# A decoder layer's feed-forward half: the sums and spills of its seven-product down projection on ScalarE's DMA queue, and a deeper buffer for its weights

## The chip, the cores and the metric

One of the eight cores of a Trainium2 chip runs the kernel. The metric is the time of one execution on the device, in microseconds (us). A core has TensorE (PE, matmuls), VectorE (DVE), ScalarE (ACT), GpSimd (POOL) and SyncE (SP). Each engine takes its instructions in a written order and waits on semaphores; transfers (DMAs) are issued here by SyncE and ScalarE, each in its own order, and run on sixteen DMA engines that all queues share.

## The reference

One decoder layer over 512 positions of width 1024: a mixer (mLSTM heads beside a gated convolution), then a feed-forward net whose hidden width is 2816. What the change touches is the end of the second half, here without the norms and the conditioning:

```python
up = causal_dwconv(u @ ffn_up[l], ffn_conv_w[l], ffn_conv_b[l])   # (512, 2 * 2816), three taps
a, gt = jnp.split(up, 2, axis=-1)
f = (jax.nn.silu(gt) * a) @ ffn_down[l]                           # (512, 2816) @ (2816, 1024)
x = x + g2 * rms_norm(f, ffn_post_g[l])
```

## The kernel before

All matmuls keep float32's accuracy by splitting both operands: ScalarE copies a 128x512 piece to a rounded high part (`hi`, line 182), and GpSimd or DVE subtracts it to get the low part (`lo`, line 183). `mm3` (line 201) then makes three matmuls for one product. `w_load` (line 190) loads 1 MB of weights by SyncE into one of two `raws` buffers and splits it into four pairs from `wpool` (20 buffers, so ten pairs).

**Up projection.** The loop over `i` runs over 22 tiles of 128 hidden channels. A tile needs four quarters of weights (`wup_0`, `wup_512`, `wup_1024`, `wup_1536`), has 48 matmuls (8 blocks of the inner dimension, three matmuls each, for two halves: the value `fa` and the gate `fg`), and ends in two PSUM banks of the four called `mm`. `conv3` (lines 969 and 971) makes the three-tap convolution, one tap on ScalarE and two on DVE; ScalarE takes the Silu of the gate (line 1043), DVE the product. The first three tiles are made earlier, in a code of their own; the loop's matmuls begin with tile 3. `u2h` and `u2l`, the split input of all up tiles, fill the buffers `uh` and `ul`.

**Down projection by seven products.** The first 18 hidden tiles go through Strassen's scheme (in Winograd's form): instead of eight products of blocks it makes seven, from sums of the blocks. A pair of hidden tiles gives the left operands: `x_` (`fx`), `r_` (`fr`) and their sums on GpSimd, `y_` (`fy`) and `q_` (`fq`). `q_` and half of `r_` are stored to device memory (`spills34`, `spilla22`) and read back later. For the right operands nine pieces of `w_down` (a list `AT` says at which up tiles) are loaded as four blocks `b` (`weight_load`), summed on DVE, GpSimd, DVE, GpSimd (`weight_sums`), and stored in `spillt1` to `spillt4` (`weight_store`). After the up projection `product` runs seven times, as p1, p2, p6, p5, p7, p3, p4: three loads of three pieces each by SyncE, then for each piece a split and 2 x 3 matmuls. `keep` copies a bank to SBUF on ScalarE (`kp`, `ku`), `put` adds it to another bank on DVE, and `back` reloads and splits `q_` (`s34`) and `r_` (`a22`). The last four hidden tiles (`wd`) are multiplied plainly, token tile by token tile, followed by the norm and the output.

**What sets the order.** SyncE and TensorE run in the order in which the code is written. For ScalarE, DVE and GpSimd a scheduler sets the order when the program is built, from its own estimate of when each operand will be ready; on the chip that order is fixed. A manual dependency of the kind `NoSync` only forces one instruction behind another on the same engine. So in the loop SyncE's queue holds, in this order, a tile's weight load, then `weight_load`, `weight_store` and the spills of earlier tiles, and a store waits there for its sum.

Of the kernel before, what the change touches and what calls it, by code (L numbers as in the profile page):

```python
# [10 lines left out]
F32 = mybir.dt.float32  # L11
F32R = mybir.dt.float32r
BF16 = mybir.dt.bfloat16
AF = mybir.ActivationFunctionType
# [3 lines left out]
P = 128  # L18
D = 1024
T = 512  # L20
KT = D // P
# [33 lines left out]
def decoder_layer(ctx, tc, w_glu0, x, c, adaT, vecs, w_glu, w_qko, w_v0, w_v, w_out, w_up, w_down, out):  # L55
    nc = tc.nc
    V, S, G, PE = nc.vector, nc.scalar, nc.gpsimd, nc.tensor
# [4 lines left out]
    raws = ctx.enter_context(tc.tile_pool(name="raws", bufs=RAWS))  # L62
    upool = ctx.enter_context(tc.tile_pool(name="upool", bufs=1))
# [24 lines left out]
    def slot(name, dt=F32):  # L88
        return slots.tile([P, T], dt, tag="t", name=name)

    def mmbank(name):
        return psum.tile([P, T], F32, tag="mm", bufs=4, name=name)
# [93 lines left out]
    def w_load(view, name, pool=None, tag="w"):  # L186

        n = view.shape[1]
        r = raws.tile([P, 2048], F32, tag="raw", name=name)
        nc.sync.dma_start(r[:, :n], view)  # L190
        return [w_split(r[:, a : min(a + T, n)], f"{name}_{a}", pool, tag) for a in range(0, n, T)]
# [105 lines left out]
    def u_tiles(name):  # L297
        hi = upool.tile([P, KT, T], F32R, tag="uh", name=f"{name}h")
        lo = upool.tile([P, KT, T], F32R, tag="ul", name=f"{name}l")
        return hi, lo, [(hi[:, j, :], lo[:, j, :]) for j in range(KT)]  # L300

    _, _, u = u_tiles("u")
# [397 lines left out]
    for j in range(KT):  # L700
# [4 lines left out]
        for d in range(1, SIDE + 1):  # L705
            t = cvs.tile([P, T], F32, tag="cvs", name=f"cs{j}_{d}")
# [134 lines left out]
    HT = T // 2  # L841
# [5 lines left out]
    def chain_sums(tt):  # L847

        ps = banks[tt]
        sq_sum(ps, msq[:, 2 * tt + 1 : 2 * tt + 2], f"mixb{tt}")  # L850
        un = adas.tile([P, D], F32, tag="ada", name=f"un{tt}")
        uns[tt] = [un[:, :T], un[:, T:]]
        V.tensor_tensor(out=uns[tt][1], in0=ps, in1=g1r[1], op=ALU.mult)
        return token_factor(msq[:, 2 * tt : 2 * tt + 2], f"rm{tt}")

    def chain_x(tt, r):

        xsq = small.tile([P, 2], F32, tag="xsq", name=f"xsq{tt}")
        for hf, m in enumerate((mg[tt], uns[tt][1])):
            V.scalar_tensor_tensor(out=x1[tt][hf], in0=m, scalar=r, in1=x1[tt][hf], op0=ALU.mult, op1=ALU.add)  # L860
            sq_sum(x1[tt][hf], xsq[:, hf : hf + 1], f"x1_{tt}_{hf}")
        for hf, un in enumerate(uns[tt]):
            V.tensor_tensor(out=un, in0=x1[tt][hf], in1=gs2r[hf], op=ALU.mult)
        return token_factor(xsq, f"rf{tt}")
# [36 lines left out]
    NE = 3  # L901
# [16 lines left out]
    with in_order():  # L918
# [3 lines left out]
        r = chain_sums(0)  # L922
        up_split(1, raw1, slots, "t")
        r = chain_x(0, r)
# [3 lines left out]
        r = chain_sums(1)  # L928
        up_split(1, raw1, slots, "t")
        r = chain_x(1, r)  # L930
# [4 lines left out]
        r = chain_sums(2)  # L935
        turn_out(1)
        r = chain_x(2, r)
# [4 lines left out]
        r = chain_sums(3)  # L942
        up_split(2, raw2, wpool, "w")
        r = chain_x(3, r)
# [29 lines left out]
    JP = 9  # L974
    NP = 2 * JP
    GJ = 3
    AT = [NE + 7 * j // 4 for j in range(JP)]
    spill = {q: dram.tile([P, JP * T], F32, tag=f"spill{q}", name=f"spill{q}") for q in ("t1", "t2", "t3", "t4", "s34", "a22")}
    sums = {}

    def weight_load(j):
        sums[j] = [slot(f"b{j}_{q}") for q in range(4)]
        for q, t in enumerate(sums[j]):
            nc.sync.dma_start(t, w_down[j][:, q * T : (q + 1) * T])

    def weight_sums(j):

        b11, b12, b21, b22 = sums[j]
        V.tensor_tensor(out=b11, in0=b12, in1=b11, op=ALU.subtract)  # L989
        G.tensor_tensor(out=b12, in0=b22, in1=b12, op=ALU.subtract)  # L990
        V.tensor_tensor(out=b22, in0=b22, in1=b11, op=ALU.subtract)
        G.tensor_tensor(out=b21, in0=b21, in1=b22, op=ALU.subtract)

    def weight_store(j):
        for q, t in zip(("t1", "t3", "t4", "t2"), sums.pop(j)):
            nc.sync.dma_start(spill[q][:, j * T : (j + 1) * T], t)

    f = {}
    af, asum, rest = [], [], []

    def split_f(src, name, wide):
        if wide:
# [8 lines left out]
    for i in range(NF):  # L1011
        if i < NE:
            pa, pg = early[i]
        else:
            pieces = w_load(w_up[i], f"wup{i}")
            if i in AT:
                weight_load(AT.index(i))
            if i - 2 in AT:
                weight_store(AT.index(i - 2))
            if i % 2 == 0 and 4 <= i < 4 + NP:  # L1020
                j = (i - 4) // 2
                x_, r_, q_ = rest[j]
                nc.sync.dma_start(spill["s34"][:, j * T : (j + 1) * T], q_)
                nc.sync.dma_start(spill["a22"][:, j * HT : (j + 1) * HT], r_[:, HT:])
            if i in (4, 8, 12, 16):
                ada_block(38 + i // 2, last_lo[0])
                ada_block(39 + i // 2, last_lo[0])
            if i == 19:
                ada_done(40, 48)
                gain(3, 40, "ffn_post_g")  # L1030
                send_rows(3 * KT, KT)
                wide = adas.tile([P, D], F32, tag="ada", name="g2r")
                g2r = row(3, lambda n: [wide[:, :T], wide[:, T:]], "g2")
            both = []
            for half in range(2):
                ps = mmbank(f"up{i}_{half}")
                for k in range(KT):
                    mm3(halves(ps), blk(pieces, half * KT + k), (u2h[:, :, k, :], u2l[:, :, k, :]), k == 0, k == KT - 1)
                both.append(ps)
            pa, pg = both  # L1040
        a = conv3(pa, i, f"fa{i}")
        g = conv3(pg, NF + i, f"fg{i}")
        S.activation(g, g, AF.Silu)
        if i >= NP:
            V.tensor_tensor(out=a, in0=a, in1=g, op=ALU.mult)
            f[i] = split_f(a, f"f{i}", False)
        else:
            if i % 2 == 0:
                x_, r_ = slot(f"fx{i}"), slot(f"fr{i}")
            cs = slice(i % 2 * HT, (i % 2 + 1) * HT)  # L1050
            V.tensor_tensor(out=x_[:, cs], in0=a[:, :HT], in1=g[:, :HT], op=ALU.mult)
            V.tensor_tensor(out=r_[:, cs], in0=a[:, HT:], in1=g[:, HT:], op=ALU.mult)  # L1052
            if i % 2:
                y_, q_ = slot(f"fy{i}"), slot(f"fq{i}")
                G.tensor_tensor(out=y_[:, :HT], in0=r_[:, :HT], in1=r_[:, HT:], op=ALU.add)  # L1055
                G.tensor_tensor(out=y_[:, HT:], in0=y_[:, :HT], in1=x_[:, :HT], op=ALU.subtract)
                G.tensor_tensor(out=q_[:, :HT], in0=x_[:, :HT], in1=r_[:, :HT], op=ALU.subtract)
                G.tensor_tensor(out=q_[:, HT:], in0=x_[:, HT:], in1=y_[:, HT:], op=ALU.subtract)
                af.append(split_f(x_, f"fx{i}", i == 1))
                asum.append(split_f(y_, f"fy{i}", i == 1))  # L1060
                rest.append((x_, r_, q_))
        if i in AT:
            weight_sums(AT.index(i))

    fsq = const.tile([P, 2 * NT], F32, name="fsq")
    banks = [[None, None] for _ in range(NT)]
    for tt, hf, make in [(2, 1, atbank), (3, 1, atbank), (0, 0, cvbank), (1, 0, cvbank), (0, 1, mmbank), (1, 1, mmbank), (2, 0, mmbank), (3, 0, mmbank)]:
        banks[tt][hf] = make(f"dn{tt}_{hf}")

    turn = [0]  # L1070

    def product(weights, left, th, hf, start, name):

        for a in range(0, JP, GJ):
            r = raws.tile([P, 2048], F32, tag="raw", name=f"{name}_{a}")
            view = weights(a)
            nc.sync.dma_start(r[:, : GJ * T].rearrange("p (j n) -> p j n", j=GJ), view)
            for n in range(GJ):
                j = a + n
                turn[0] += 1  # L1080
                w = w_split(r[:, n * T : (n + 1) * T], f"{name}_{j}", eng=V if turn[0] % 2 else G)
                hi, lo, off = left(j)
                for q in range(2):
                    ts = slice(off + q * P, off + (q + 1) * P)
                    mm3(banks[2 * th + q][hf], (hi[:, ts], lo[:, ts]), w, start and j == 0, j == JP - 1, True)
# [17 lines left out]

    def back(q, a, n, name):
        t = slot(f"{name}r")
        nc.sync.dma_start(t[:, :n], spill[q][:, a : a + n])
        hi, lo = slot(f"{name}h", F32R), slot(f"{name}l", F32R)
        S.activation(hi[:, :n], t[:, :n], AF.Copy)
        G.tensor_tensor(out=lo[:, :n], in0=t[:, :n], in1=hi[:, :n].bitcast(F32), op=ALU.subtract)
        return hi, lo  # L1110
# [7 lines left out]
    s34 = [back("s34", j * T, T, f"s34_{j}") for j in range(JP)]  # L1118
# [5 lines left out]
    a22 = [back("a22", a * HT, min(T, (JP - a) * HT), f"a22_{a}") for a in range(0, JP, 2)]  # L1124
# [9 lines left out]
    for tt in range(NT):  # L1134
# [12 lines left out]
        r = token_factor(fsq[:, 2 * tt : 2 * tt + 2], f"ro{tt}")  # L1147
# [70 lines left out]
```

## Time and profile before

| | |
|---|---|
| median of three runs | 861.71 us (861.38 to 867.46) |
| profiled execution | 867.5 us, of which the span is 865.8 us |
| mean granted clock of TensorE | 0.961 |
| busy: PE, DVE, ACT, POOL | 801.4, 526.7, 403.4, 499.4 us |
| DMA | 140.01 MB, mean 162 GB/s |
| SyncE's queue (q1) and ScalarE's (q10) | 116.26 and 23.08 MB |

In the rows of the profile a name such as `wup_0h<-wup` reads output <- input with buffer numbers left out, and `L182` is a line of the kernel. A row of the list of waits gives who waited, for whom, then us in total, how often, and the longest. A row of the timeline gives the start, the duration, the engine, the instruction, and in brackets the idle time before it and what ended it. A busy TensorE is not one at its peak, since its matmuls are pipelined; the distance between the starts of matmuls is what counts.

### The profile page before, as it was taken

How to read it: one execution, taken by the hardware profiler on the slowest of the kernel's cores; microseconds unless marked ns; L12 is line 12 of the kernel's file. 1: busy time of each engine (PE TensorE's matmuls, PEld its weight loads, DVE VectorE, ACT ScalarE, POOL GpSimd, SP SyncE). 2: the span in 40 equal slices, each digit the busy share in tenths (PEclk: the TensorE clock that was granted, in tenths of full speed). 3: DMA queues.
4: the chain of work that ended last, by engine and by line, in shares of the span. 5: the costliest groups of instructions: out<-in, count | busy, mean ns of one | idle time of the engine just before them, and what ended most of it. 6: DMA issues, size and time to landing. Idle time of an engine off the chain costs nothing.

```text
span 865.8 us, 10702 instructions
## 1 busy us (share of the span) xinstructions
PE 801.4 (93%) x3732; PEld 656.3 (76%) x3732; DVE 526.7 (61%) x824; ACT 403.4 (47%) x758; POOL 499.4 (58%) x414
## 2 busy tenths in 40 slices
PE   8999999999999999999999677797987899979996
PEld 5788887787888888888898565686766688858765
DVE  6679999999974345486877524535533335423334
ACT  6684466676645547423442233324233344544341
POOL 4799767786875325447131557357466482465661
PEclk9999999999999999999999788988989999998999
DMA  8953222121272315195367563345634353646444
GB/s 314 344 221 111 97 98 98 50 98 49 86 230 98 122 50 195 52 375 217 134 204 210 205 211 124 135 175 170 249 116 144 124 176 115 207 153 226 160 155 170
DMA packets 43897, 140.01 MB, mean 162 GB/s; under 512 B 4770, under 2 KB 6082, under 8 KB 37572
## 3 DMA queue, kind: packets, MB, share of 16 engines
q1 hardware_dynamic: 35748, 116.26, 38.4%
q10 hardware_dynamic: 8096, 23.08, 7.6%
q8 instruction: 29, 0.48, 0.2%
q14 instruction: 24, 0.20, 0.1%
HBM read 122.13 MB, written 17.19 MB: 161 GB/s over the span
## 4 chain that ended last, share of the span: by engine, by line
PE 65%; POOL 9%; issue 8%; DVE 8%; DMA 6%; ACT 4%; POOLq 0%; DVEq 0%; ACTq 0%; SPq 0%
PE up L201 18%; PE qko L201 12%; PE dn L201 8%; PE glu L201 6%; PE mixa L201 5%; PE mixb L201 5%; DMA ada<-in_adaT 3%; PE v L201 3%; PE s L513 2%; DVE cv L715 2%; PE o L524 1%; PE glu L344 1%; POOL wup_0l L183 1%; DMA p<-spillt 1%; DVE junk L167 1%
## 5 line engine op out<-in xcount | busy, mean ns | idle before, releaser
L715 DVE SCALAR_TENSOR_TENSOR cv<-gt,cvw,cv 128x502 f32<-128x502 f32 (+24 forms) x200 | 134.4, 727 | 1.9 <-ACT cv L703 1.3
L201 PE MATMUL up<-u2h,wup_0h 128*128 128x512 f32 (+1 forms) x100 | 43.7, 437 | 29.1 <-ACT wup_0h L182 29.1
L201 PE MATMUL up<-u2h,wup_0l 128*128 128x512 f32 (+1 forms) x100 | 44.6, 446 | 10.7 <-POOL wup_0l L183 10.7
L201 PEld LDWEIGHTS up<-u2h,wup_0h 128*128 128x128 f32 x100 | 22.6, 226 | 35.9 <-ACT wup_0h L182 32.5
L711 POOL TENSOR_TENSOR cs<-cs,cs 128x510 f32<-128x510 f32 (+3 forms) x32 | 42.7, 1337 | 4.7 <-ACT cs L709 4.7
L201 PE MATMUL up<-u2l,wup_0h 128*128 128x512 f32 (+1 forms) x100 | 42.6, 426 | 0.2 <-DVE u2l L884 0.2
L183 POOL TENSOR_TENSOR wup_0l<-wup,wup_0h 128x512 fp32r<-128x512 f32 x20 | 27.8, 1389 | 19.5 <-ACT wup_0h L182 19.5
L1055 POOL TENSOR_TENSOR fy<-fr 128x256 f32<-128x256 f32 x9 | 8.8, 978 | 51.9 <-DVE fr L1052 51.9
L201 PE MATMUL up<-u2h,wup_512h 128*128 128x512 f32 (+1 forms) x100 | 38.0, 380 | 0.0
L201 PE MATMUL up<-u2l,wup_512h 128*128 128x512 f32 (+1 forms) x100 | 37.5, 375 | 0.0
L201 PEld LDWEIGHTS up<-u2h,wup_0l 128*128 128x128 f32 x100 | 22.8, 228 | 19.2 <-POOL wup_0l L183 15.2
L201 PE MATMUL up<-u2h,wup_512l 128*128 128x512 f32 (+1 forms) x100 | 37.2, 372 | 0.0
L167 DVE SCALAR_TENSOR_TENSOR junk<-ada,cb 128x1024 bf16<-128x1024 f32 x20 | 29.2, 1459 | 12.1 <-DMA ada<-in_adaT 12.0
L201 PE MATMUL up<-u2h,wup_1024h 128*128 128x512 f32 (+1 forms) x100 | 36.4, 364 | 0.0
L201 PE MATMUL up<-u2h,wup_1536h 128*128 128x512 f32 (+1 forms) x100 | 36.4, 364 | 0.0
L201 PE MATMUL up<-u2l,wup_1536h 128*128 128x512 f32 (+1 forms) x100 | 36.4, 364 | 0.0
L201 PE MATMUL up<-u2h,wup_1024l 128*128 128x512 f32 (+1 forms) x100 | 36.4, 364 | 0.0
L201 PE MATMUL up<-u2h,wup_1536l 128*128 128x512 f32 (+1 forms) x100 | 36.3, 363 | 0.0
L201 PE MATMUL up<-u2l,wup_1024h 128*128 128x512 f32 (+1 forms) x100 | 36.3, 363 | 0.0
L183 POOL TENSOR_TENSOR wqko_1024l<-wqko,wqko_1024h 128x512 fp32r<-128x512 f32 x12 | 15.6, 1298 | 25.1 <-PE v L201 15.1
L990 POOL TENSOR_TENSOR b<-b,b 128x512 f32<-128x512 f32 x9 | 11.5, 1282 | 29.1 <-DVE b L989 29.1
L709 ACT ACTIVATE cs<-gt,cvw 128x511 f32<-128x511 f32 (+4 forms) x40 | 27.1, 712 | 1.5 <-POOL cs L711 1.0
(1024 smaller groups left out, 2772.4 us busy)
## 6 DMA issues: line engine op xcount, KB each, us to landing
wup<-in_w_up SPq DMA_DIRECT2D x22, 1024.0 KB, 5.2
wqko<-in_w_qko SPq DMA_DIRECT2D x12, 1024.0 KB, 4.8
ada<-in_adaT ACTq DMA_DIRECT2D x20, 512.0 KB, 5.5
b<-in_w_down SPq DMA_DIRECT2D x36, 256.0 KB, 6.6
spillt<-b SPq DMA_DIRECT2D x36, 256.0 KB, 2.0
p<-spillt SPq DMA_DIRECT2D x12, 768.0 KB, 5.5
ada<-in_adaT SPq DMA_DIRECT2D x16, 512.0 KB, 6.6
wo<-in_w_out SPq DMA_DIRECT2D x8, 1024.0 KB, 10.3
```

What stands on the lines that cost most here:

```text
L167: t = V.scalar_tensor_tensor(out=junk, in0=r, scalar=1.0, in1=cb, op0=ALU.mult, op1=ALU.mult, accum_out=mod[:, i : i + 1])
L183: (eng or G).tensor_tensor(out=lo[:, :n], in0=src, in1=hi[:, :n].bitcast(F32), op=ALU.subtract)
L201: PE.matmul(ps, l, r, start=start and i == 0, stop=stop and i == 2, skip_group_check=again)
L344: PE.matmul(ps, blk(wk, i)[a], u[k][b], start=k == 0 and p == 0, stop=k == KT - 1 and p == 1)
L513: PE.matmul(sp[:, :n], ks[d][:, cc * P : (cc + 1) * P], qs[d][:, cc * P :], start=d == 0, stop=d == 1)
L524: PE.matmul(o[:, : DH + 2], E[h][cc][:, a : a + P], vs[h][cc], start=cc == 0, stop=cc == tt)
L709: S.activation(t[:, d:], cvx[j][:, : T - d], AF.Copy, scale=w(CK - 1 - d))
L711: G.tensor_tensor(out=side[:, d:], in0=side[:, d:], in1=t[:, d:], op=ALU.add)
L715: last_tap = V.scalar_tensor_tensor(out=cp[:, d:], in0=cvx[j][:, : T - d], scalar=w(CK - 1 - d), in1=cp[:, d:], op0=ALU.mult, op1=ALU.add)
L990: G.tensor_tensor(out=b12, in0=b22, in1=b12, op=ALU.subtract)
L1055: G.tensor_tensor(out=y_[:, :HT], in0=r_[:, :HT], in1=r_[:, HT:], op=ALU.add)
```

## The change

The loads, stores and spills that belong to the seven products move from SyncE's queue to ScalarE's, each written at the place where its data arises and not two or more tiles later. `weight_load` is forced behind the last tile's Silu on ScalarE (`anchor`). `AT` becomes three tiles of every four from 6 to 16. `back` reloads through ScalarE's queue as well. `product` takes its first two loads into `raws` and all later ones into a ring of four buffers cut from `uh` and `ul`, which are free when the last up matmul has read `u2h` and `u2l`. The arithmetic is the same.

```diff
-    AT = [NE + 7 * j // 4 for j in range(JP)]
+    AT = [6, 7, 8, 10, 11, 12, 14, 15, 16]
+    def behind(ins, anchor):
+        tc.add_manual_dep(ins.ins, anchor.ins.name, mybir.DependencyInfo(mybir.DependencyClass.NoSync, mybir.DependencyReason.DATA),
+                          reason="order on an engine")
...
     def weight_load(j):
...
-            nc.sync.dma_start(t, w_down[j][:, q * T : (q + 1) * T])
+            behind(nc.scalar.dma_start(t, w_down[j][:, q * T : (q + 1) * T]), anchor[0])
...
     def weight_store(j):
         for q, t in zip(("t1", "t3", "t4", "t2"), sums.pop(j)):
-            nc.sync.dma_start(spill[q][:, j * T : (j + 1) * T], t)
+            nc.scalar.dma_start(spill[q][:, j * T : (j + 1) * T], t)
...
             if i in AT:
                 weight_load(AT.index(i))
-            if i - 2 in AT:
-                weight_store(AT.index(i - 2))
-            if i % 2 == 0 and 4 <= i < 4 + NP:
-                j = (i - 4) // 2
-                x_, r_, q_ = rest[j]
-                nc.sync.dma_start(spill["s34"][:, j * T : (j + 1) * T], q_)
-                nc.sync.dma_start(spill["a22"][:, j * HT : (j + 1) * HT], r_[:, HT:])
...
-        S.activation(g, g, AF.Silu)
+        anchor[0] = S.activation(g, g, AF.Silu)
...
-                rest.append((x_, r_, q_))
+                j = i // 2
+                nc.scalar.dma_start(spill["s34"][:, j * T : (j + 1) * T], q_)
+                nc.scalar.dma_start(spill["a22"][:, j * HT : (j + 1) * HT], r_[:, HT:])
         if i in AT:
             weight_sums(AT.index(i))
+            weight_store(AT.index(i))
...
-    turn = [0]
+    turn, at = [0], [0]
+    ring = [upool.tile([P, KT, T], F32, tag=tag, name=f"ring{tag}").rearrange("p j t -> p (j t)") for tag in ("uh", "ul")]
+    rings = [z[:, a : a + 2048] for a in (0, 2048) for z in ring]
...
-            r = raws.tile([P, 2048], F32, tag="raw", name=f"{name}_{a}")
+            r = rings[at[0] % len(rings)] if at[0] > 1 else raws.tile([P, 2048], F32, tag="raw", name=f"{name}_{a}")
+            at[0] += 1
...
     def back(q, a, n, name):
         t = slot(f"{name}r")
-        nc.sync.dma_start(t[:, :n], spill[q][:, a : a + n])
+        nc.scalar.dma_start(t[:, :n], spill[q][:, a : a + n])
```

How the built order moves is seen at three places. First SyncE in the middle of the up projection, from tile 11's weight load (`wup11`) on. Before, with the loads and stores of the sums (`b`, `spillt`) between the weight loads:

```order
L190 DMA wup11_5379<-in_w_up 128x2048
L984 DMA b5_0_5397<-in_w_down 128x512
L984 DMA b5_1_5398<-in_w_down 128x512
L984 DMA b5_2_5399<-in_w_down 128x512
L984 DMA b5_3_5400<-in_w_down 128x512
L190 DMA wup12_5484<-in_w_up 128x2048
L996 DMA spillt1_4528<-b4_0_5298 128x512
L996 DMA spillt3_4530<-b4_1_5299 128x512
L996 DMA spillt4_4531<-b4_2_5300 128x512
L996 DMA spillt2_4529<-b4_3_5301 128x512
L1023 DMA spills34_4532<-fq9_5267 128x512
L1024 DMA spilla22_4533<-fr8_5180 128x256
```

and in the change, from the same load:

```order
L190 DMA wup11_5369<-in_w_up 128x2048
L190 DMA wup12_5480<-in_w_up 128x2048
L190 DMA wup13_5585<-in_w_up 128x2048
L190 DMA wup14_5680<-in_w_up 128x2048
L190 DMA wup15_5777<-in_w_up 128x2048
```

Weight loads of the up projection now follow each other with nothing between.

Second, ScalarE around the split of tile 11's weights. Before, where the splits of tiles 11 and 12 (`wup11`, `wup12`) stand behind the convolution and the Silu of tile 10's gate (`fg10c`):

```order
L969 ACTIVATE fa10c_5362<-up10_0_5312,vec_108 128x512
L1007 ACTIVATE fy9h_5276<-fy9_5266 128x512
L969 ACTIVATE fg10c_5366<-up10_1_5337,vec_108 128x512
L1043 ACTIVATE fg10c_5366<-fg10c_5366 128x512
L182 ACTIVATE wup11_0h_5381<-wup11_5379 128x512
L182 ACTIVATE wup11_512h_5385<-wup11_5379 128x512
L182 ACTIVATE wup11_1024h_5389<-wup11_5379 128x512
L182 ACTIVATE wup11_1536h_5393<-wup11_5379 128x512
L182 ACTIVATE wup12_0h_5486<-wup12_5484 128x512
L182 ACTIVATE wup12_512h_5490<-wup12_5484 128x512
```

and in the change, from the first split of tile 11 on, with the loads (`b2`) of the third piece of weight sums:

```order
L182 ACTIVATE wup11_0h_5371<-wup11_5369 128x512
L989 DMA b2_0_5090<-in_w_down 128x512
L989 DMA b2_1_5091<-in_w_down 128x512
L989 DMA b2_2_5092<-in_w_down 128x512
L1061 DMA spills34_4532<-fq7_5049 128x512
L989 DMA b2_3_5093<-in_w_down 128x512
L969 ACTIVATE fg8c_5160<-up8_1_5131,vec_108 128x512
L182 ACTIVATE wup11_512h_5375<-wup11_5369 128x512
L1001 DMA spillt1_4528<-b2_0_5090 128x512
L182 ACTIVATE wup11_1024h_5379<-wup11_5369 128x512
```

The first split of tile 11 now stands ahead of tile 8's gate convolution, and the load and store of the sums stand among the splits; the store `spillt1` waits for DVE's first sum.

Third, ScalarE between the third product (p6) and the fourth (p5). Before, the splits of p5 stand behind the copies `ku20` and `ku21`, which need p6's last matmul:

```order
L1096 ACTIVATE ku20_6729<-dn2_1_6427 128x512
L1096 ACTIVATE ku21_6730<-dn3_1_6428 128x512
L1108 ACTIVATE s34_6h_6771<-s34_6r_6769 128x512
L1108 ACTIVATE s34_7h_6777<-s34_7r_6775 128x512
L1108 ACTIVATE s34_8h_6783<-s34_8r_6781 128x512
L182 ACTIVATE p5_0h_6789<-p5_0_6787 128x512
L182 ACTIVATE p5_1h_6799<-p5_0_6787 128x512
L182 ACTIVATE p5_2h_6809<-p5_0_6787 128x512
```

and in the change, from p5's fifth piece to p7's first:

```order
L182 ACTIVATE p5_4h_6824<-ringuh_6435 128x512
L1111 DMA s34_4r_6752<-spills34_4532 128x512
L182 ACTIVATE p5_5h_6834<-ringuh_6435 128x512
L182 ACTIVATE p5_6h_6845<-ringul_6436 128x512
L1113 ACTIVATE s34_4h_6754<-s34_4r_6752 128x512
L182 ACTIVATE p5_7h_6855<-ringul_6436 128x512
L1111 DMA s34_5r_6758<-spills34_4532 128x512
L182 ACTIVATE p5_8h_6865<-ringul_6436 128x512
L1101 ACTIVATE ku20_6724<-dn2_1_6427 128x512
L182 ACTIVATE p7_0h_6880<-ringuh_6435 128x512
```

All of p5's splits now stand ahead of the copies, and the reloads of s34 and their splits are spread among them.

More of the change, by code (lines that the diff above doesn't have):

```diff
@@ L995, in weight_store @@
         for q, t in zip(("t1", "t3", "t4", "t2"), sums.pop(j)):
-            nc.sync.dma_start(spill[q][:, j * T : (j + 1) * T], t)
+            nc.scalar.dma_start(spill[q][:, j * T : (j + 1) * T], t)
     f = {}
-    af, asum, rest = [], [], []
+    af, asum = [], []
+    anchor = [None]
     def split_f(src, name, wide):
```

## The prediction

> **What bounds the kernel now.** I read the page first, for the engine that carries the chain, then the stages of the feed-forward half, then the waits of TensorE there, then one wait in order of time.
>
> ```profile
> span 865.8 us, 10702 instructions
> ...
> PE 65%; POOL 9%; issue 8%; DVE 8%; DMA 6%; ACT 4%; POOLq 0%; DVEq 0%; ACTq 0%; SPq 0%
> ```
>
> TensorE has most of the chain, but a third of it lies elsewhere. The next view gives the busy time by stage: first to last matmul of up tiles 3 to 21, the seven products, the first 9.9 us of the closing products, the rest, and last a stretch of two up tiles without a wait.
>
> ```profile
> 464.30:735.40 271.10, 231.28 (x915) 183.86 (x914) 120.91 (x168) 97.61 (x161) 152.06 (x130) 0.90 0.47 163
> 735.40:832.50 97.10, 88.88 (x380) 72.17 (x378) 37.05 (x38) 45.59 (x82) 57.45 (x42) 0.96 0.57 194
> 832.50:842.40 9.90, 7.74 (x26) 3.90 (x25) 1.57 (x3) 3.28 (x7) 9.26 (x8) 1.00 0.20 80
> 842.40:865.80 23.40, 16.48 (x73) 13.31 (x71) 11.32 (x19) 5.18 (x16) 2.19 (x4) 0.93 0.46 157
> 603.30:625.00 21.70, 21.70 (x98) 17.96 (x97) 11.68 (x16) 7.04 (x11) 12.14 (x12) 1.00 0.76 274
> ```
>
> The columns are the stretch, its length, the busy us (and instructions) of TensorE, its weight loads, DVE, ScalarE and GpSimd, then granted clock, DMA share and GB/s. No other engine is near full in the up stage, and the DMA engines are half idle (0.47). The last row shows that TensorE can run there without a gap at clock 1.00 while 274 GB/s move. So it is held by waits, and TensorE's own waits name them:
>
> ```profile
> PE up L201 <- ACT wup_0h L182: 29.1, 8, 4.2
> PE up L201 <- POOL wup_0l L183: 10.7, 8, 5.5
> PE dn L201 <- POOL p_0l L183: 5.5, 2, 3.9
> PE dn L201 <- ACT p_0h L182: 2.8, 1, 2.8
> ```
>
> Eight times an up tile's first quarter of weights isn't split when TensorE comes to it. Tile 11 stands for all eight (rows of SyncE, ScalarE, TensorE and GpSimd in order of time, with the page's landing time for such a load):
>
> ```profile
> wup<-in_w_up SPq DMA_DIRECT2D x22, 1024.0 KB, 5.2
> ...
> 566.51 0.33 SPq L190 DMA_DIRECT2D wup<-in_w_up  x1
> 587.17 0.78 ACT L969 ACTIVATE fg10c<-up,vec 128x512 f32<-128x512 f32 x1 [3.69 <-PE up L201]
> 589.61 0.63 ACT L1043 ACTIVATE fg10c<-fg10c 128x512 f32<-128x512 f32 x1 [1.66 <-DVE fg10c L971]
> 590.15 0.61 ACT L182 ACTIVATE wup_0h<-wup 128x512 fp32r<-128x512 f32 x1
> 586.75 0.39 PE L201 MATMUL up<-u2h,wup_1536l 128*128 128x512 f32 x1
> 590.81 0.80 PE L201 MATMUL up<-u2h,wup_0h 128*128 128x512 f32 x1 [3.68 <-ACT wup_0h L182]
> 592.93 0.80 PE L201 MATMUL up<-u2h,wup_0l 128*128 128x512 f32 x1 [0.90 <-POOL wup_0l L183]
> 604.97 0.39 PE L201 MATMUL up<-u2h,wup_0h 128*128 128x512 f32 x1
> 615.85 0.39 PE L201 MATMUL up<-u2h,wup_0h 128*128 128x512 f32 x1
> ```
>
> The load was issued at 566.51 and, at 5.2 us, had landed by 572. ScalarE split it at 590.15, 18 us later: in its written order the split stands behind tile 10's second convolution and its Silu, which end only after tile 10's matmuls. The wait is one of order, not of transfer. It costs more than its 3.68 us: tile 11 takes 604.97 - 590.81 = 14.16 us, and the next, without a wait, 615.85 - 604.97 = **10.88 us**.
>
> **The change, part by part.** *Up stage.* SyncE keeps only the weight loads of the up projection there; the 72 loads and stores of the sums and the 18 spills go to ScalarE's queue. With that the scheduler writes ScalarE's splits elsewhere: tile 11's first split now stands ahead of tile 8's second convolution, more than two tiles before TensorE needs it. All 19 tiles at 10.88 us are 206.7 us; the stage took 271.1. Gain if no wait is left: **64.4 us**, eight times 8.05 (39.8 / 8 = 5.0 waited, the rest lost at the lowered clock, 0.90 over the stage).
>
> What it adds to ScalarE is issuing. The nearest rows on its queue (min/median/max of an issue in ns), the landing times, and the other engines' shares in the sums:
>
> ```profile
> L960 ACTq DMA_DIRECT2D x1d<-x x8: 326/327/333, 413.2 to 436.8; - x8
> L826 ACTq DMA_DIRECT2D x<-in_x x8: 334/442/489, 368.4 to 376.7; - x8
> ...
> x<-in_x ACTq DMA_DIRECT2D x8, 256.0 KB, 6.1
> b<-in_w_down SPq DMA_DIRECT2D x36, 256.0 KB, 6.6
> spillt<-b SPq DMA_DIRECT2D x36, 256.0 KB, 2.0
> L183 POOL TENSOR_TENSOR wup_512l<-wup,wup_512h 128x512 fp32r<-128x512 f32 x18 | 24.3, 1352 | 0.0
> L989 DVE TENSOR_TENSOR b<-b,b x9: 682/686/1771, 479.0 to 677.2; 128x512 f32<-128x512 f32 x9
> L990 POOL TENSOR_TENSOR b<-b,b 128x512 f32<-128x512 f32 x9 | 11.5, 1282 | 29.1 <-DVE b L989 29.1
> L1055 POOL TENSOR_TENSOR fy<-fr 128x256 f32<-128x256 f32 x9 | 8.8, 978 | 51.9 <-DVE fr L1052 51.9
> ```
>
> Between 0.33 and 0.44 us an issue; I take 0.44, that of several in a row. A tile with sums then asks ScalarE for four splits at 0.6, two convolutions at 0.78, a Silu and a split of the product at 0.63, together 5.3 us, and nine issues, 4.0 us: 9.3 of 10.88 us. Nine of the tiles 6 to 17 have sums, three need only some 5.7. GpSimd has four splits at 1.35, half a pair's sums (four operations of at most 0.98 for two tiles, 2.0) and two weight sums at 1.28: 10.0 at most with sums, 7.4 without, 112 of 131 us over the twelve. Both fit, without much room.
>
> The new waits stand at ScalarE: a store waits for DVE's or GpSimd's sum, and the first sum for loads that ScalarE issued a few instructions before. Behind that store stand the next splits, the convolution and the Silu; DVE waits for the convolution (and holds its own next convolution behind the sum that waits for the load), TensorE for the split two tiles on. A load lands in 2.0 (the bound below, from the store row) to 6.6 us, with two to four instructions in between. That leaves 0 to 4 us of waiting a tile, and I take 2, nearer to 6.1 less some 4: 11.3 us a tile with sums. Over twelve tiles that is 9 x 0.4 late and 3 x 5 of slack, so no lasting delay. At 4 us it is 9 x 2.4 = 22 less 15, a lag of 7. Two leads cover a lag: ten quarters of split weights (wpool's 20 buffers, 27 us of matmuls), and the PSUM banks of two tiles, which leave a convolution a tile and a half, 16 us. I charge nothing; without the cover each late tile costs some 8 us as now.
>
> That the sums now start at tile 6 and not 3 leaves the first three tiles without them; the last store, about tile 18, is read by the third product, over four tiles later.
>
> Bandwidth: the stage's 163 GB/s over 271 us are 44 MB; in 207 us, 214 GB/s, below the 274 that ran beside matmuls at full rate.
>
> *Products.* The second part in order of time:
>
> ```profile
> 735.41 0.39 PE L201 MATMUL dn<-p_0h,fx 128*128 128x512 f32 x1
> 747.69 0.39 PE L201 MATMUL dn<-p_0h,fx 128*128 128x512 f32 x1
> 771.80 1.28 ACT L1096 ACTIVATE ku<-dn 128x512 f32<-128x512 f32 x2 [9.97 <-PE dn L201]
> 774.53 0.62 ACT L182 ACTIVATE p_0h<-p 128x512 fp32r<-128x512 f32 x1
> 779.58 0.79 PE L201 MATMUL dn<-p_0l,fy 128*128 128x512 f32 x1 [3.88 <-POOL p_0l L183]
> 807.93 0.50 PE L201 MATMUL dn<-p_0l,s_0h 128*128 128x512 f32 x1 [1.58 <-POOL p_0l L183]
> 832.48 0.39 PE L201 MATMUL dn<-wd_0h,f18h 128*128 128x512 f32 x1
> 842.39 0.39 PE L201 MATMUL dn<-wd_0h,f18h 128*128 128x512 f32 x1
> 847.84 0.39 PE L201 MATMUL dn<-wd_0h,f18h 128*128 128x512 f32 x1
> ```
>
> One product is 747.69 - 735.41 = 12.28 us (1.36 for each of nine pieces), seven are 86.0; they took 832.48 - 735.41 = 97.1. Lost: **11.1 us**, most of it where p5's splits stand behind the copies ku, which wait 9.97 us for the end of a product. In the new order all nine splits of p5 stand ahead of those copies, and four ring buffers besides two keep loads ahead. The ring is free only when the last up matmul ends, so the third load starts then; TensorE has six pieces in hand, 6 x 1.36 = 8.2 us, against some 4.4 to 6.6 for the landing and 1.9 for a split (0.62 on ScalarE, 1.28 on GpSimd). Covered; without the cover a short wait. The reloads of s34 and a22 make ScalarE wait at their splits, a few us each at most, while its splits may run ten pieces (13.6 us) ahead.
>
> *Closing products.* The first token tile took 842.39 - 832.48 = 9.91 us, the second 5.45: GpSimd was still splitting wd (busy 9.26 of 9.90 in the stage view). These loads now go to buffers that have been free since the first product, and their splits are paced by p4's matmuls. Gain: **4.5 us**. What is late next is nothing but TensorE; the tail after it stays.
>
> *Sum.* The profiled execution took 867.5 us, of which 1.7 lies around the span. 867.5 - 64.4 - 11.1 - 4.5 = 787.5. I add 1.6 for one short wait like that at 807.93: **789 us**. That execution is the slowest of the three shown; the median is 861.71, so 5.8 us of it may be no part of the kernel's usual time, and the result may as well be 783.
>
> **Rivals.** *ScalarE falls behind* (chance 0.15): loads on its queue land later than 6.6 us or GpSimd's sums hold the stores, the lead is used up by tile 12, and four of the later tiles wait. At 2.4 us of delay and 3.3 for the clock (14.16 less 10.88) each, 23 us: 811. For it: the 9.3 of 10.88 us. Against it: three tiles of slack.
>
> *Only the up stage gains* (0.10): the reloads' waits at ScalarE take the place of the copies' wait in the products: 787.5 + 11.1 + 1.6, 800.
>
> *No change* (0.03): both queues feed the same transfers, loads land no sooner, and the splits stay late: 862 to 867. Against it: the 18 us between landing and split. The Trainium skill, "DMA: Bandwidth & Descriptors", section "Issuing engines are not separate DMA queues", speaks for this rival: issuing from several engines saves only the sequencer's time. By that rule the sum would be near 0, since SyncE's issuing is on no path; the trace doesn't contradict it on bandwidth, but bandwidth isn't what TensorE waits for.
>
> *Slower* (0.04): each of the nine tiles with sums makes ScalarE wait out its own chain: load, four sums, store. With nothing between, that is 9.3 + 6.6 + 3.9 (two sums on DVE at 0.68 and two on GpSimd at 1.28) = 19.8 us a tile, 8.9 above 10.88, and 3.3 for the clock: nine times 12.2 is 110, and 787.5 + 110 = 897. It decides against the change from (80 - 9 x 3.3) / 9 = 5.6 us above 10.88, that is 16.5 us a tile.
>
> **How the numbers follow.** Forecast 0.68 (783 to 795), the rivals 0.15, 0.10, 0.03 and 0.04. The range goes from 779 (783 less the doubt of 4 in the terms) to 812, which takes in both smaller gains. Faster by over 1%, about what a measurement of this kernel can tell from no change: 0.68 + 0.15 + 0.10 = 0.93; within 1%: 0.03; slower: 0.04.
>
> **What would show it.** In the trace after, TensorE's waits for wup_0h and wup_0l should be gone or below 5 us in sum, up tiles 3 to 21 should last about 207 us at clock 1.00, the products 86 to 88, the first closing tile 5.5. ScalarE should wait for DVE and GpSimd at the stores, some 2 us a tile. Waits of TensorE from tile 12 on, growing, would mean the first rival; a wait at s34's or a22's split the second.

## The result

The changed kernel takes 790.64 us (median of four, 789.48 to 792.1), the kernel before 861.91 in the same session (861.38 to 867.46): a ratio of 0.916, 95% interval 0.912 to 0.920. The forecast was 789.

The page of the changed kernel, its span and its chain of work:

```profile
span 788.9 us, 10687 instructions
...
PEclk9999999999999999999999999999999999999999
...
PE 78%; DVE 9%; DMA 6%; ACT 3%; issue 2%; POOL 1%; ACTq 0%; DVEq 0%; SPq 0%; POOLq 0%
```

TensorE's share of the chain went from 65 to 78%, GpSimd's from 9 to 1, that of "issue" from 8 to 2, and the granted clock stays at nine tenths or more in every slice. The stages, with the columns that the prediction explains (up tiles 3 to 21, seven products, first closing token tile, rest):

```profile
464.42:674.16 209.74, 207.40 (x915) 171.15 (x914) 130.47 (x164) 93.02 (x152) 152.10 (x126) 1.00 0.61 203
674.16:760.07 85.91, 85.91 (x380) 70.95 (x378) 48.26 (x43) 50.04 (x91) 71.10 (x49) 1.00 0.72 247
760.07:765.51 5.44, 5.44 (x26) 4.50 (x24) 1.38 (x3) 0.00 (x0) 2.17 (x2) 1.00 0.00 0
765.51:788.90 23.39, 16.48 (x73) 13.33 (x71) 11.52 (x20) 5.51 (x16) 2.21 (x4) 0.92 0.46 157
```

Against 271.1, 97.1, 9.9 and 23.4 us in the profiled execution of the kernel before (its slowest, 867.46 us), the stages gain 61.4, 11.2, 4.5 and nothing. TensorE, 231.28 us busy in the up stage before, is now 207.40 for the same matmuls: the waits had cost time in the matmuls too, at a granted clock of 0.90. Its waits after 440 us are only two, of another kind than before:

```profile
PE up L201 <- DVE fa17c L971: 1.2, 1, 1.2
PE up L201 <- DVE fa15c L971: 1.2, 1, 1.2
```

Tile 11, the prediction's example, in order of time (ScalarE, then TensorE):

```profile
531.65 0.62 ACT L182 ACTIVATE wup_0h<-wup 128x512 fp32r<-128x512 f32 x1
534.53 0.78 ACT L969 ACTIVATE fg8c<-up,vec 128x512 f32<-128x512 f32 x1 [2.26 <-issue]
551.49 0.39 PE L201 MATMUL up<-u2h,wup_0h 128*128 128x512 f32 x1
```

Its first split stands ahead of tile 8's second convolution and is made 19.8 us before TensorE comes for it; before, it came 0.66 us ahead of a matmul that had waited 3.68 us.

### The profile page after: what moved, and what is told of

Read it like the earlier page. It is cut to its first block, busy times and chain, and to the rows that moved or that the text cites. A ratio compares the mean times of both kernels' runs of the same rounds, so it can differ in the third digit from the quotient of the medians.

```text
span 788.9 us, 10687 instructions
## 1 busy us (share of the span) xinstructions
PE 772.3 (98%) x3732; PEld 643.1 (82%) x3732; DVE 550.5 (70%) x824; ACT 403.6 (51%) x758; POOL 511.8 (65%) x414
## 4 chain that ended last, share of the span: by engine, by line
PE 78%; DVE 9%; DMA 6%; ACT 3%; issue 2%; POOL 1%; ACTq 0%; DVEq 0%; SPq 0%; POOLq 0%
PE up L201 26%; PE dn L201 13%; PE qko L201 10%; PE glu L201 7%; PE mixa L201 6%; PE mixb L201 5%; PE glu L344 4%; DVE cv L715 4%; PE v L201 3%; DMA b<-in_w_down 2%; PE s L513 2%; DMA ada<-in_adaT 1%; PE o L524 1%; DMA wqko<-in_w_qko 1%; DMA vec<-in_vecs 1%
## 5 line engine op out<-in xcount | busy, mean ns | idle before, releaser
L201 PE MATMUL up<-u2h,wup_0h 128*128 128x512 f32 (+1 forms) x100 | 36.6, 366 | 2.3 <-DVE fa17c L971 1.2
L201 PE MATMUL up<-u2l,wup_0h 128*128 128x512 f32 (+1 forms) x100 | 36.5, 365 | 0.2 <-DVE u2l L884 0.2
L167 DVE SCALAR_TENSOR_TENSOR junk<-ada,cb 128x1024 bf16<-128x1024 f32 x20 | 32.0, 1599 | 6.5 <-DMA ada<-in_adaT 6.3
L201 PE MATMUL up<-u2h,wup_0l 128*128 128x512 f32 (+1 forms) x100 | 36.4, 364 | 0.0
L201 PE MATMUL up<-u2h,wup_512h 128*128 128x512 f32 (+1 forms) x100 | 36.4, 364 | 0.0
L183 POOL TENSOR_TENSOR wup_0l<-wup,wup_0h 128x512 fp32r<-128x512 f32 x20 | 27.4, 1369 | 11.2 <-ACT wup_0h L182 11.2
L183 POOL TENSOR_TENSOR wup_1024l<-wup,wup_1024h 128x512 fp32r<-128x512 f32 x20 | 26.7, 1335 | 10.8 <-ACT wup_1024h L182 10.8
L183 POOL TENSOR_TENSOR wup_512l<-wup,wup_512h 128x512 fp32r<-128x512 f32 x20 | 27.4, 1369 | 8.0 <-ACT wup_512h L182 8.0
L182 ACT ACTIVATE wup_0h<-wup 128x512 fp32r<-128x512 f32 x22 | 13.8, 627 | 34.7 <-POOL b L995 11.0
L183 POOL TENSOR_TENSOR wup_1536l<-wup,wup_1536h 128x512 fp32r<-128x512 f32 x20 | 28.6, 1432 | 3.2 <-PE up L201 2.2
```

Source lines behind the costliest of these rows:

```text
L167: t = V.scalar_tensor_tensor(out=junk, in0=r, scalar=1.0, in1=cb, op0=ALU.mult, op1=ALU.mult, accum_out=mod[:, i : i + 1])
L182: S.activation(hi[:, :n], src, AF.Copy)
L183: (eng or G).tensor_tensor(out=lo[:, :n], in0=src, in1=hi[:, :n].bitcast(F32), op=ALU.subtract)
L201: PE.matmul(ps, l, r, start=start and i == 0, stop=stop and i == 2, skip_group_check=again)
```

## The experiments

### The up stage: the queues, or the order they bring about

The queues changed and with them ScalarE's written order. Two runs part the two; a third keeps only the loads on SyncE. The edits are shown in short, with `...` where code is left out. First, the new queues with the old order:

```diff
 pieces = w_load(w_up[i], f"wup{i}")        # wacts: the splits on ScalarE
...
+if i % 2 and i >= 5:
+    behind(wacts[0], anchor[0])
```

> The changed kernel with every transfer on the queue that the change gave it, but the first split of each odd up tile from 5 on pinned on ScalarE behind the Silu of the tile before, which makes ScalarE's written order that of the kernel before (two tiles' splits in a row, then two tiles' convolutions). Theory (order of the splits is the cause, the queues only bring it about): the waits for wup_0h are back, eight or nine of them at 7 to 8 us each, up tiles 3 to 21 take 262 to 275 us, products and closing stay at 86 and 5.4, total 843 to 858. Rival (the transfers run better from two queues, order matters little): up tiles 209 to 220 us, total 790 to 801.

Measured: 863.6 us, ratio to before 0.9996 (0.9976 to 1.0016). The time is that of the kernel before, some 6 us above the theory's 858. TensorE's waits, the stages (up, products, closing), and tile 11 again (ScalarE, DVE and TensorE in order of time):

```profile
PE up L203 <- ACT wup_0h L184: 39.4, 9, 5.6
PE up L203 <- POOL wup_0l L185: 12.0, 8, 2.8
```

```profile
464.59:747.21 282.62, 231.13 (x916) 182.69 (x914) 119.78 (x166) 95.17 (x153) 147.07 (x125) 0.89 0.44 150
747.21:833.11 85.90, 85.90 (x379) 70.95 (x378) 46.24 (x41) 50.44 (x90) 74.07 (x52) 1.00 0.71 247
833.11:838.55 5.44, 5.44 (x25) 4.50 (x24) 1.38 (x3) 0.00 (x0) 1.02 (x1) 1.00 0.00 0
```

```profile
578.63 0.78 ACT L971 ACTIVATE fg10c<-up,vec 128x512 f32<-128x512 f32 x1 [3.68 <-DMA b<-in_w_down]
579.65 0.69 DVE L996 TENSOR_TENSOR b<-b,b 128x512 f32<-128x512 f32 x1 [3.52 <-issue]
580.26 1.53 DVE L973 SCALAR_TENSOR_TENSOR fg10c<-up,vec,fg10c 128x511 f32<-128x511 f32 x2
581.88 0.63 ACT L1047 ACTIVATE fg10c<-fg10c 128x512 f32<-128x512 f32 x1 [2.47 <-DVE fg10c L973]
582.41 0.61 ACT L184 ACTIVATE wup_0h<-wup 128x512 fp32r<-128x512 f32 x1
583.08 0.79 PE L203 MATMUL up<-u2h,wup_0h 128*128 128x512 f32 x1 [4.49 <-ACT wup_0h L184]
```

The split stands behind the Silu again, and TensorE waits 4.49 us. The up stage takes 282.6 us, more than the 271.1 of before and than the theory's 262 to 275, and this takes back what products and closing keep of the change. The waits for wup_0h are 39.4 us against 29.1. There are nine and not eight, and the chain behind some of them is longer: at tile 10 DVE makes a sum of weights (0.69 us) ahead of the gate's two taps, the Silu waits 2.47 us for DVE and not 1.66, and TensorE's wait is longer by the same 0.81 us.

Then the other way round: the old queues, tiles of sums and buffers, with the splits early.

```diff
+for n in (i + 1, i + 2):                   # from tile 4 on
+    if n < NF and n not in ahead and i >= 4:
+        ahead[n] = w_load(w_up[n], f"wup{n}"); heads[n] = list(wacts)
...
 a = conv3(pa, i, f"fa{i}")
-g = conv3(pg, NF + i, f"fg{i}")
+g = conv3(pg, NF + i, f"fg{i}", heads[i + 2][0])   # pinned behind this split
```

> The kernel before with all its queues, its tiles of sums and its buffers, but the load and splits of an up tile written two tiles ahead, and the second convolution of each tile pinned on ScalarE behind the first split of the tile two later. Theory (order): the 18 us between landing and split go, up tiles 3 to 21 take 207 to 222 us, the products (97) and the closing stage (9.9) stay, total 798 to 815. Rival (SyncE's queue itself holds the loads back, since stores wait in it): the loads land late and ScalarE now waits for them ahead of its convolutions, up tiles 245 us or more, total 836 to 880.

Measured: 813.74 us, ratio 0.943 (0.940 to 0.945). Tiles 3 to 5, ahead of the pins, then 6 to 21, the products and the first closing tile:

```profile
461.26:506.48 45.22, 35.07 (x146) 27.97 (x145) 25.33 (x37) 16.74 (x29) 28.36 (x25) 0.92 0.47 147
506.48:680.72 174.24, 174.24 (x771) 144.15 (x769) 106.35 (x130) 79.03 (x132) 127.01 (x106) 1.00 0.61 213
680.72:777.20 96.48, 89.45 (x379) 72.61 (x378) 37.25 (x38) 45.84 (x83) 57.83 (x42) 0.95 0.58 197
777.20:786.86 9.66, 7.73 (x26) 3.88 (x25) 1.59 (x3) 3.04 (x7) 9.04 (x8) 1.00 0.16 60
```

Sixteen tiles take 174.24 us, 10.89 each, TensorE busy throughout, with every load and store of the sums in SyncE's queue. The order is the cause. This run also writes the weight loads two tiles earlier in SyncE's queue; with that, the queue, stores and all, doesn't hold them back. Products and closing stage stay as they were.

The third run asks what in SyncE's queue made the scheduler write the splits late. The loads of b alone go back:

```diff
-behind(nc.scalar.dma_start(t, w_down[j][:, q * T : (q + 1) * T]), anchor[0])
+nc.sync.dma_start(t, w_down[j][:, q * T : (q + 1) * T])
```

> The changed kernel with the 36 loads of the sums' weights back on SyncE's queue; its stores and reloads stay on ScalarE's. The written order has tiles 7, 9, 11, 13, 15 and 17 split behind the Silu of the tile before again. Theory (order, set by whether anything else is written between the weight loads on SyncE): six waits at 7 to 8 us, up tiles 250 to 260 us, total 832 to 842. Rival (it is the stores, which wait for sums at the head of SyncE's queue, that held the weight loads): no wait, 788 to 797.

Measured: 833.85 us, ratio 0.966 (0.964 to 0.968). TensorE's waits:

```profile
PE up L201 <- ACT wup_0h L182: 24.6, 6, 4.1
PE up L201 <- POOL wup_0l L183: 4.1, 6, 1.0
```

Six waits, as many as the order has late tiles; the up stage takes 254.3 us. Loads on SyncE are enough for the late order; the stores need not be there.

### Products and closing: the ring, or the order

The ring of buffers alone, on the kernel before:

```diff
+rings = [z[:, a : a + 2048] for a in (0, 2048) for z in ring]   # ring: the tiles uh, ul
-r = raws.tile([P, 2048], F32, tag="raw", name=f"{name}_{a}")
+r = rings[at[0] % len(rings)] if at[0] > 1 else raws.tile(...)
```

> The kernel before with the six buffers for the products' loads alone (the four freed by the up projection and the two of before), all queues as before. The written order still has the splits of p5 behind the copies ku2. Theory: the closing stage goes from 9.9 to 5.4 us, the products keep most of their 11 us, the up stage is unchanged: total 852 to 858. Rival (the prediction's reading that the ring gives the products their 11 us as well): 845 to 848.

Measured: 856.2 us, ratio 0.992 (0.989 to 0.995). Up stage, products and closing stage:

```profile
463.56:730.93 267.37, 228.35 (x916) 181.40 (x914) 120.45 (x165) 95.58 (x158) 151.20 (x129) 0.91 0.45 158
730.93:824.28 93.35, 88.28 (x379) 72.23 (x378) 45.85 (x40) 51.76 (x90) 71.92 (x50) 0.96 0.64 227
824.28:829.72 5.44, 5.44 (x25) 4.50 (x24) 1.38 (x3) 0.00 (x0) 0.00 (x0) 1.00 0.00 0
```

The ring gives the closing stage its 4.5 us and the products 3.7 of 11.1; the up stage (first row), which it doesn't touch, is as before but for 3.7 us. The opposite, the changed kernel without the ring:

```diff
-r = rings[at[0] % len(rings)] if at[0] > 1 else raws.tile(...)
+r = raws.tile([P, 2048], F32, tag="raw", name=f"{name}_{a}")
```

> The changed kernel without the four ring buffers: all product weights go through the two buffers of before. Its written order still has the splits of p5 ahead of the copies ku2. Theory (the products' 11 us are the reloads' place in the order, the ring gives only the closing stage its 4.5): up 209 to 211 us, products 86 to 88, first closing tile 9.5 to 10, total 794 to 797. Rival (the prediction's reading that the ring's buffers keep the loads ahead and give the products their 11 us too): products 92 to 97, total 800 to 806.

Measured: 799.3 us, ratio 0.927 (0.924 to 0.930), between the two expectations:

```profile
672.14:763.88 91.74, 88.64 (x379) 70.29 (x378) 38.91 (x41) 45.72 (x85) 63.65 (x43) 1.00 0.63 207
763.88:773.68 9.80, 7.71 (x25) 3.88 (x24) 2.20 (x4) 3.65 (x8) 9.18 (x8) 1.00 0.19 67
```

The closing stage loses its 4.4 us and the products 5.8, in their last three. So neither part alone gives the products their 11; the last of these runs adds to the ring the order of p5 without moving a reload:

```diff
-u2 = keep(1, 1, "ku2")                     # ahead of p5
...
 product(summed("t1"), ..., "p5")
+u2 = keep(1, 1, "ku2", wacts[-1])          # pinned behind p5's last split
```

> The kernel before with the ring buffers alone (as in the run with the ring), and the two copies ku2 pinned on ScalarE behind the last of p5's nine splits; the reloads stay on SyncE. In the run with the ring alone the products took 93.4 us, and the waits stood at p5's first splits. Theory (the rest of the products' loss is the written order of p5's splits and ku2): products 86 to 88 us, closing 5.4, up stage as before: total 848 to 852. Rival (the reloads' place on SyncE's queue, where they and the products' loads wait for one another): products 91 to 95, total 854 to 859.

Measured: 846.18 us, ratio 0.980 (0.977 to 0.983), some 2 us below the theory's total. Up stage and products:

```profile
463.54:732.68 269.14, 229.43 (x916) 182.24 (x914) 119.27 (x166) 96.05 (x158) 150.47 (x129) 0.90 0.46 158
732.68:819.11 86.43, 86.15 (x379) 70.89 (x378) 48.99 (x40) 51.47 (x90) 73.42 (x50) 1.00 0.69 245
```

With ring and order they take 86.4 us while the reloads stay on SyncE, against 85.9 in the changed kernel. All but 0.5 us of what the reloads' queue gives is thus the order that it brings about.

### ScalarE's lag

The two waits left in the up stage are for PSUM banks that ScalarE and DVE free late. Tile 16's first half of matmuls ends 5.44 us after its start:

```profile
605.89 0.39 PE L201 MATMUL up<-u2h,wup_0h 128*128 128x512 f32 x1
625.64 0.76 ACT L969 ACTIVATE fa16c<-up,vec 128x512 f32<-128x512 f32 x1
```

So its convolution starts 625.64 - 611.33 = 14.3 us late, where tile 6's starts 1.3 us late. Four runs looked for the reason, with the changed kernel beside the first two:

> The changed kernel once more, to have its time from the same session as the next three: 789 to 792 us, with two waits of TensorE for PSUM banks of some 1.2 us each in the last up tiles.

Measured: 789.39 us (787.99 to 790.14), one PSUM wait of 1.0 us in its trace.

```diff
 if i in AT:
     weight_sums(AT.index(i))
-    weight_store(AT.index(i))
+if i - 1 in AT:
+    weight_store(AT.index(i - 1))
```

> The changed kernel with the four stores of each tile's sums written one up tile later; loads, sums and queues as they are. Theory (ScalarE falls 15 us behind because its stores wait for sums that DVE and GpSimd have only begun): its waits for b, some 30 us between 497 and 640, fall below 10, its second convolutions run at most 6 us behind TensorE, and the two PSUM waits go: 787 to 789 us, 1.5 to 3 us below the changed kernel of the same session. Rival (it is the issues themselves and the waits for the load's landing, since DVE still holds the convolution behind the sum): the lag stays at 10 us or more, 790 to 792.

Measured: 789.35 us. This tells nothing of the theory: in the trace ScalarE's instructions of the up stage stand in the order of the changed kernel, so the line moved in the code moved none of them, and it is one more run of that kernel.

```diff
-AT = [6, 7, 8, 10, 11, 12, 14, 15, 16]
+AT = [5, 6, 8, 9, 11, 12, 14, 15, 17]
```

> The changed kernel with the nine tiles of sums spread out: [5, 6, 8, 9, 11, 12, 14, 15, 17] in place of [6, 7, 8, 10, 11, 12, 14, 15, 16], so that a tile without sums follows every two and not every three. In the trace of the changed kernel the lag of ScalarE grew by some 5 us in each round of three tiles with sums and one without. Theory (a plain balance of work on ScalarE): it grows by at most 2 us a round here, the peak is 10 us or less, the PSUM waits go: 787 to 789 us. Rival (the lag comes from a single event, or tile 17's sums come too late to be made up): 790 to 792.

Measured: 789.14 us, ratio 0.915 (0.912 to 0.918). The lag grew from 5.3 us at tile 6 to 14.1 at tile 18, 2.2 a round where at most 2 were expected, but it started from 5.3 and not from 1.3 us, since the sums begin a tile earlier, and ended as high. Two waits, 1.0 us together: no change that can be measured, so the balance of the tiles isn't shown to be the reason.

Then the sums themselves. This kernel leaves them out and stores the four blocks as they were loaded, so its result is another one, and only its time is of use:

```diff
-weight_sums(AT.index(i))
```

> The changed kernel without the 36 sums of weights: loads and stores stay, but the four blocks are stored as they were loaded. Theory (the lag comes from the chain load, four sums, store on which ScalarE waits): lag at most 5 us, no PSUM wait, total 786 to 788.5. Rival (issues and landing of the loads alone make it): the lag still peaks at 10 us or more, total 788.5 to 791.

Measured: 786.62 us, ratio 0.912 (0.909 to 0.915), no wait of TensorE. Tile 16:

```profile
604.74 0.39 PE L201 MATMUL up<-u2h,wup_0h 128*128 128x512 f32 x1
615.47 0.76 ACT L969 ACTIVATE fa16c<-up,vec 128x512 f32<-128x512 f32 x1
```

A lag of 615.47 - 610.18 = 5.3 us, 6.2 at the most, a little above the theory's 5. Last, the loads of b on GpSimd's queue:

```diff
-behind(nc.scalar.dma_start(t, ...), anchor[0])
+nc.gpsimd.dma_start(t, ...)
```

> The changed kernel with the 36 loads of the sums' weights on GpSimd's queue; stores and reloads stay on ScalarE's. The written order keeps each tile's splits two tiles early. Theory (nothing but weight loads on SyncE gives the early order, whichever other queue takes the loads): up tiles 207 to 212 us, total 787 to 792, and ScalarE's lag, relieved of four issues a tile, peaks at 5 to 10 us instead of 14. Rival (GpSimd, at 10 of 10.88 us a tile, is overrun by some 1.8 us of issuing): waits for wup_0l from tile 10 on, total 795 to 815.

Measured: 787.42 us, ratio 0.913 (0.911 to 0.915), no wait of TensorE, up stage 206.9 us, lag 9.1 at the most. GpSimd had room for 36 issues, and the early order comes with either of the two queues that were tried in SyncE's place. So the lag is made by ScalarE's stores standing behind sums, and by its own loads ahead of them: either taken away, it is no longer long enough to reach TensorE. The run without sums takes work from DVE and GpSimd too; the next run leaves it to them and moves only loads and stores.

### What they point to

In the second run, with the sums' loads and stores on SyncE and the early order by pins, ScalarE's convolutions start 0.2 to 0.3 us behind TensorE from tile 6 to 19. So the last run takes that kernel, its early loads and pins from the first tiles on, and adds to it the ring and the reloads on ScalarE:

```diff
-    if n < NF and n not in ahead and i >= 4:
+    if NE <= n < NF and n not in ahead and i >= 1:
...
+r = rings[at[0] % len(rings)] if at[0] > 1 else raws.tile(...)
-nc.sync.dma_start(t[:, :n], spill[q][:, a : a + n])
+nc.scalar.dma_start(t[:, :n], spill[q][:, a : a + n])
```

> What the experiments point to: the kernel before with its sums' loads and stores on SyncE, the up weights' loads and splits written two tiles ahead from tile 3 on with each tile's second convolution pinned behind the first split of the tile two later, the six buffers for the products' loads, and only the reloads of s34 and a22 on ScalarE's queue. Theory (order alone for the up stage, reloads plus ring for the products and the closing stage, and no lag since ScalarE neither issues nor waits for the sums): up tiles 3 to 21 take 207 to 210 us without a PSUM wait, the lag of the first convolutions stays below 2 us, products 86, first closing tile 5.4: 784 to 789 us, 0 to 5 below the changed kernel. Rival (stores at the head of SyncE's queue hold the weight loads once nothing else is slow): waits for wup_0h, 792 or more.

Measured: 788.53 us (785.99 to 789.42), ratio 0.914 (0.911 to 0.916).

```profile
463.00:671.89 208.89, 207.19 (x915) 171.16 (x914) 130.41 (x168) 92.03 (x154) 151.39 (x127) 1.00 0.58 200
671.89:757.80 85.91, 85.91 (x380) 70.96 (x379) 45.28 (x40) 50.85 (x90) 72.87 (x50) 1.00 0.71 247
757.80:763.24 5.44, 5.44 (x26) 4.50 (x25) 1.38 (x3) 0.00 (x0) 0.18 (x1) 1.00 0.00 0
```

Convolutions again start 0.2 to 0.3 us behind TensorE from tile 7 to 19, with the sums still made by DVE and GpSimd, and one wait of 1.7 us is left at tile 6. It is as fast as the changed kernel and no faster by anything that shows: its interval and that of the changed kernel in its second session (0.912 to 0.917) overlap, as does that of the run with the loads on GpSimd. The 2.4 us that the lag costs are 0.3% of the time.

## Why the prediction was right, and where not

*The up stage* (64.4 forecast, 61.4 measured): right in cause and nearly in size. That order was the cause is shown both ways: the old order costs all of it with the new queues, the new order gives it with the old ones from tile 6 on. The 3 us short are the two PSUM waits (2.4) and 0.5 of matmul time beside them (207.40 us busy, 206.90 in the runs without a wait).

*No lasting delay of ScalarE* is the step that failed. The prediction took 2 us of waiting in a tile with sums, 4 as the bound, and 5 us of slack in a tile without. By that a round of three tiles with sums and one without leaves no lag, and at the bound 2.2 us (3 x 2.4 less 5). Measured as above, the lag was 1.3 us at tile 6, 5.7 at 10, 11.0 at 14 and 14.3 at 16, so a round added 4.4 to 5.3 us. ScalarE's idle time between 497 and 640 us, the five longest rows for its own sums and loads, then two for other steps:

```profile
ACT wup_0h L182 <- POOL b L995: 11.0, 3, 4.3
ACT wup_0h L182 <- DMA b<-in_w_down: 9.8, 3, 4.1
ACT wup_512h L182 <- POOL b L997: 4.9, 2, 2.5
ACT wup_1024h L182 <- POOL b L995: 4.3, 3, 1.9
ACT wup_0h L182 <- DVE b L996: 3.8, 2, 2.1
```

```profile
ACT wup_512h L182 <- DVE fa15c L971: 3.0, 1, 3.0
ACT fx15h L1013 <- DVE fr L1051: 2.2, 1, 2.2
```

All rows that name sums, loads or stores are 43.3 us. Idle time here includes issuing, which the prediction had counted apart; without some 17 us of it 26 are left, 2.9 for each of the nine tiles, more than the 2 taken and less than the bound. The issues themselves took 0.47 us on average, near the 0.44 taken. The other rows are 42 us, 27 without issues, and DVE's steps of ScalarE's own tile are the largest part (20.3). This the prediction put at nothing, and it took all time beside work and issues for slack. How the lag divides between these terms no run shows. That its cause is the sums' loads and stores in ScalarE's queue is shown: 14.3 us with both there, 9.1 and 6.2 at the most without the loads or without the sums, 0.2 to 0.3 from tile 7 on with neither.

The first rival, ScalarE falling behind, was thus half right: its mechanism is there, and it cost 2.4 us and not 23. There were two waits of 1.2 us, for PSUM banks at tiles 17 and 19, and not four of 2.4. The tiles with sums end at 16, just as the lag comes near the 16 us that the PSUM banks cover, and the clock took nothing: it is 1.00 over the stage. (The 3.3 us that the rivals charge for the clock, 14.16 less 10.88, also hold 0.90 us of waiting for wup_0l.) The 1.6 us that the sum held for one short wait happened to cover most of it.

*Products* (11.1 forecast, 11.2 measured): right in size, and the split of it was not stated. The ring alone gave 3.7, the reloads alone 5.4, ring and p5's order together 10.7 with the reloads left where they were. The second rival, reloads' waits in place of the copies', didn't come: TensorE has no gap there.

*Closing* (4.5 and 4.5): right, and it is the ring's; the runs with the ring have 5.44 us, those without 9.7 to 9.9.

*The total* (789 forecast, 790.64 measured) is nearer than its terms, in part by luck. The terms and the sum start from the profiled execution of the kernel before, the slowest of four: it lies 76.5 us above the profiled one of the changed kernel, while the medians lie 71.3 apart (74.2 in the second session). Its up stage took 271.1 us, and 267.4 and 269.1 us in the two runs with the ring that leave this stage alone, so some 2 to 4 us of the 61.4 may be no part of the gain. From the median the same terms give the 783 that the prediction named beside 789, and that would have been over 7 us short.

*No change*, with the rule of the Trainium skill ("DMA: Bandwidth & Descriptors", section "Issuing engines are not separate DMA queues"): the rule itself agrees with the runs, and still the time fell. The new queues with the old order were as slow as the old ones, and the old queues with the early order ran the 16 tiles at 10.89 us. What the rule doesn't speak of is that the choice of the queue changed where the scheduler put another engine's instructions.

## What to carry to other kernels

When an engine waits for a buffer that had landed long before, look at what stands ahead of the instruction that makes it ready: that is an order to be changed, and the transfers can stay. Moving transfers to another queue can do this as a side effect. Loads written early enough and a pin behind the one instruction do it without another queue, and a pin that brings the old order back tells which of the two it was. On an engine that runs in written order, price a new wait by the whole chain behind it (load, sums, store) and not by the landing of the load alone, and compare the lag that it builds up with the smallest buffer between that engine and the one that sets the time.

## What the runs showed of the hardware

DVE's sums b at line 996 took 1.76 us in the median in the changed kernel and 0.69 in the kernel of the last run, where the same operation is line 995 (min/median/max in ns; the changed kernel first):

```profile
L996 DVE TENSOR_TENSOR b<-b,b x9: 692/1759/1768, 517.1 to 638.8; 128x512 f32<-128x512 f32 x9
```

```profile
L995 DVE TENSOR_TENSOR b<-b,b x9: 691/692/694, 481.3 to 629.4; 128x512 f32<-128x512 f32 x9
```

One of the long ones beside what GpSimd does then, in the changed kernel:

```profile
542.36 1.77 DVE L996 TENSOR_TENSOR b<-b,b 128x512 f32<-128x512 f32 x1 [1.92 <-POOL b L995]
542.28 1.30 POOL L183 TENSOR_TENSOR wup_1536l<-wup,wup_1536h 128x512 fp32r<-128x512 f32 x1
```

GpSimd's subtraction began 0.08 us earlier and ends at 543.58; DVE's ends 0.55 us after that, at 544.13, a little less than the 0.69 it needs alone. In the last run's kernel no instruction of GpSimd ran beside any of the 18 sums of DVE, and all took 0.67 to 0.69 us. The Trainium skill, "SBUF — State Buffer", section "Who interferes with whom", says that a DVE instruction with two inputs in SBUF contends with a GpSimd instruction that reads SBUF, and calls the pair of ports that they share an exclusive lock. These rows agree with it. The prediction had priced these sums at 0.68 us; the difference lies in the chain that made ScalarE late, though no run took it away by itself.
